# Layer 0's up-projection in seven products of halves instead of eight, and modulation units of 256 columns

## The chip, the cores and the metric

One core of one Trainium2 chip runs the kernel. Its engines are TensorE (PE in the rows; PEld is its weight load), VectorE (DVE), ScalarE (ACT), GpSimd (POOL) and SyncE (SP, which here issues DMAs). The metric is the device time of one execution in microseconds; the kernel before took 2715.18 us in the median of three runs (2710.06 to 2716.42).

## The reference

Two layers of a diffusion backbone in f32, on 512 latent and 256 context tokens with 1024 features. A layer modulates and norms the input, projects it, runs three mixers (mLSTM, attention, gated DeltaNet), merges them, and ends with a gated MLP. The change rewrites the first product of that MLP in layer 0:

```python
D_MODEL = 1024
D_FF = 2816
...
def conv_ffn(xn, w_up, conv_w, w_down):
    u = dwconv(xn @ w_up, conv_w)
    a, gt = jnp.split(u, 2, axis=-1)
    return (a * jax.nn.silu(gt)) @ w_down
...
        m_lat = jnp.split((silu_c @ ada_w[l] + ada_b[l])[:, None, :], 6, axis=-1)
```

`dwconv` is a convolution of width 3 along the tokens, on each sequence by itself. The last line is the modulation: a vector of 6 x 1024 values for a layer, for the latent tokens and for the context.

## The kernel before

Activations lie with features on the 128 partitions and tokens along the free axis, 768 of them in layer 0 (512 latent, 256 context) and 512 in layer 1's MLP. f32 products are made from pairs: each operand is split into a high part (`xh`, `wh`: ScalarE's cast to f32r) and a low one (`xl`, `wl`: what is left, VectorE's subtraction, L205), and TensorE adds three products, high by high, low by high and high by low (`mm3`, L248 to L250). `wsplit` makes the pair of a weight tile after `wraw` has loaded it through SP; raw tiles go round in a ring of three, pairs in a ring of two.

`ffn` (layer 0: names f0...) takes the 22 blocks of 128 hidden features in pairs. A unit f0g02 is the gate half of blocks 2 and 3 of group 0, f0a02 the other half of the same blocks; `gemm_fm` makes such a unit block by block: 8 row blocks of weights by 3 matmuls, each over 512 and over 256 tokens. The first unit, f0g00, goes its own way (`gemm_first`), f0a00 is the second and f0g02 the third. When a block is ready, `conv` takes it out of PSUM: ScalarE scales the middle tap (L1708), VectorE adds the two others (L1709, L1711, `scalar_tensor_tensor`). A gate block then gets silu (L1717); an a block is multiplied by its gate on GpSimd (L1723), cast to `gh` on ScalarE (L1724), and split to `gl` on VectorE (L1725). After four blocks the down-projection of the group (f0d0, f0d4, ...) follows one unit late: the order on TensorE is g00, a00, g02, a02, g40, d0, a40, g42, a42, g80, d4 and so on. It has eight output blocks, each of 4 row blocks by 3 matmuls by 512 and 256 tokens, and VectorE adds the result to the residual `hr` (L1743).

The modulation of layer 1 and of layer 0's MLP is made in units of 128 columns between other work (`ada_unit`): eight small matmuls of 32x128 into four row groups (`adp`, L467), a copy on ScalarE (`adr`, L470), and one unit later a transpose (`adc`, L489) and VectorE's sum (L491). 80 of the 96 units are made so. In layer 0's MLP sixteen of them follow the first blocks.

The order of the program is the scheduler's: it takes the instructions by priority and by an estimate of when they can start, each engine then runs its list in order, and semaphores make it wait. Weight loads and splits have a raised priority. GpSimd's and SP's lists are in order as well: what waits there holds back all behind it.

In the mLSTM a masked query `qz` is loaded for each tile of 128 tokens into one of two buffers, multiplied on GpSimd (L998) and read by the last matmuls of the tile (L1013).

```python
                        nc.vector.scalar_tensor_tensor(out=a[:, s + 1:e], in0=ps[:, 0:n - 1], scalar=w[0],
                                                       in1=a[:, s + 1:e], op0=ALU.mult, op1=ALU.add)
```

Here `ps` is a PSUM tile, so one of the two inputs lies in SBUF.

## Time and profile before

| | before |
|---|---|
| median of three runs | 2715.18 us |
| profiled execution, and its span | 2712.51 us, 2710.7 us |
| mean granted clock of TensorE | 0.994 |
| TensorE busy | 2640.8 us, 97% |
| VectorE, ScalarE, GpSimd busy | 1576.0, 1000.3, 267.0 us |
| chain that ended last | 84% TensorE, 7% DMA, 6% VectorE |
| layer 0's MLP | about 1012 to 1600 us of the span |

The busy share of TensorE says that its work makes the time; the table by stage says where it is full. A row of the timeline gives an instruction's start and duration in us; on TensorE durations overlap, since matmuls are pipelined, so the distance between two starts is what one costs. A duration on VectorE or GpSimd includes what the instruction waited after its semaphores had been met.

### The profile page before, as it was taken

Reading aid. Unit: us, or ns where it says so; the run is one execution under the profiler, and the core shown is the slowest. Engines: PE = TensorE matmul, PEld = TensorE weight load, DVE = VectorE, ACT = ScalarE, POOL = GpSimd, SP = SyncE. Lnnn points to the kernel's source line nnn. Section 1 sums busy time; section 2 is a strip of 40 time slices with the busy share of each in tenths; the row PEclk is TensorE's granted clock in tenths of the full one; section 3 lists DMA queues with packets and bytes.
Section 4 is the critical chain, followed back from the end, with each engine's and each line's share of the span. In section 5 each row is a group of like instructions: output and inputs, shape, how many; then the busy total and the mean of one; then the engine's idle time right before and its main releaser. Section 6 shows DMA issues by size and latency. Waiting matters only on the chain.

```text
span 2710.7 us, 46057 instructions
## 1 busy us (share of the span) xinstructions
PE 2640.8 (97%) x18041; PEld 2252.5 (83%) x18041; DVE 1576.0 (58%) x3517; ACT 1000.3 (37%) x2269; POOL 267.0 (10%) x262
## 2 busy tenths in 40 slices
...
DMA packets 526187, 344.29 MB, mean 127 GB/s; under 512 B 48167, under 2 KB 491281, under 8 KB 525201
## 3 DMA queue, kind: packets, MB, share of 16 engines
...
q8 instruction: 142, 2.33, 0.3%
...
q14 instruction: 76, 0.62, 0.1%
...
## 4 chain that ended last, share of the span: by engine, by line
PE 84%; DMA 7%; DVE 6%; ACT 1%; issue 1%; SPq 1%; POOL 0%; ACTq 0%; DVEq 0%; POOLq 0%
PE mg04p L248 2%; PE mg04p L250 2%; PE mg04p L249 2%; PE adp L467 2%; PE y0p L248 1%; PE y0p L249 1%; PE y0p L250 1%; PE mg14p L248 1%; PE mg14p L250 1%; PE mg14p L249 1%; PE y1p L248 1%; PE y0op L248 1%; PE y0op L250 1%; PE y0op L249 1%; PE y1p L249 1%
## 5 line engine op out<-in xcount | busy, mean ns | idle before, releaser
L1723 POOL TENSOR_TENSOR f0a<-f0a,f0g 128x768 f32<-128x768 f32 x22 | 40.6, 1848 | 486.4 <-DVE f0a L1711 486.4
L467 PE MATMUL adp<-ad,s 128*32 128x128 f32 x1280 | 66.8, 282 | 4.4 <-DVE cz0t L904 2.4
L1723 POOL TENSOR_TENSOR f1a<-f1a,f1g 128x512 f32<-128x512 f32 x22 | 28.5, 1294 | 313.3 <-DVE f1a L1711 303.5
L467 PEld LDWEIGHTS adp<-ad,s 128*32 128x32 f32 x1280 | 34.1, 109 | 28.1 <-issue 9.5
L1725 DVE TENSOR_TENSOR f0gl<-f0a,f0gh 128x768 fp32r<-128x768 f32 x22 | 21.1, 958 | 61.4 <-ACT f0gh L1724 61.3
L1724 ACT CAST f0gh<-f0a 128x768 fp32r<-128x768 f32 x22 | 18.4, 835 | 80.0 <-POOL f0a L1723 80.0
L1647 POOL TENSOR_TENSOR y0a<-y0a,y0g 128x768 f32<-128x768 f32 x16 | 33.0, 2063 | 128.0 <-DVE y0g L1644 125.7
L902 ACT ACTIVATE mg0t<-mg04p 128x512 f32<-128x512 f32 (+1 forms) x40 | 19.4, 486 | 40.6 <-PE mg04p L250 31.9
L470 ACT COPY adr<-adp 128x128 f32<-128x128 f32 x80 | 21.2, 265 | 33.4 <-PE adp L467 32.8
L1647 POOL TENSOR_TENSOR y1a<-y1a,y1g 128x512 f32<-128x512 f32 x16 | 23.9, 1494 | 75.6 <-DVE y1g L1644 75.3
L1717 ACT ACTIVATE f0g<-f0g 128x768 f32<-128x768 f32 x22 | 18.5, 846 | 32.9 <-DVE f0g L1711 32.9
L998 POOL TENSOR_TENSOR m0qz<-m0qz,m0e 64x512 f32<-64x512 f32 x12 | 15.4, 1282 | 151.9 <-DMA m0e<-g0rd 115.2
L1644 DVE SCALAR_TENSOR_TENSOR y0g<-y0g,y0p 128x512 f32<-128x512 f32 (+1 forms) x32 | 17.4, 550 | 15.4 <-PE y0p L250 14.6
L1717 ACT ACTIVATE f1g<-f1g 128x512 f32<-128x512 f32 x22 | 13.8, 632 | 32.9 <-DVE f1g L1711 32.9
L491 DVE TENSOR_REDUCE ada<-adc 128x2 f32<-128x8 f32 x80 | 12.9, 161 | 21.6 <-PE adc L489 21.3
L987 DVE SCALAR_TENSOR_TENSOR m0mb<-m0mb,g0a,cst 128x128 f32<-128x128 f32 x48 | 14.1, 346 | 18.7 <-DMA m0mb<-g0rd 18.6
L1668 DVE SCALAR_TENSOR_TENSOR hr<-y0op,y0gh,hr 128x512 f32<-128x512 f32 (+1 forms) x16 | 9.8, 615 | 21.1 <-PE y0op L250 21.1
L489 PE MATMUL adc<-cst,adr 128*128 128x128 f32 x80 | 21.9, 273 | 0.0
L1620 DVE TENSOR_TENSOR y0l<-y0ld,y0h 128x768 fp32r<-128x768 f32 x12 | 13.0, 1093 | 12.6 <-ACT y0h L1619 12.5
L1011 PE MATMUL m0n<-m0vb,m0mb 128*128 128x129 f32 x96 | 18.1, 279 | 1.2 <-issue 1.2
L1743 DVE SCALAR_TENSOR_TENSOR hr<-f0d4p,ada,hr 128x512 f32<-128x512 f32 (+1 forms) x16 | 9.9, 618 | 15.7 <-PE f0d4p L250 15.7
L1743 DVE SCALAR_TENSOR_TENSOR hr<-f0d8p,ada,hr 128x512 f32<-128x512 f32 (+1 forms) x16 | 9.9, 618 | 15.7 <-PE f0d8p L250 15.7
...
## 6 DMA issues: line engine op xcount, KB each, us to landing
...
```

The source lines that it names most:

```text
L248: nc.tensor.matmul(o, hv[:, k, :], xh[:, k, :], start=(k == 0), stop=False)
L249: nc.tensor.matmul(o, hv[:, k, :], xl[:, k, :], start=False, stop=False)
L250: nc.tensor.matmul(o, lv[:, k, :], xh[:, k, :], start=False, stop=(k == nk - 1))
L467: nc.tensor.matmul(ps[32 * j:32 * j + 32, 0:128], self.s32[:, 2 * k:2 * k + 32], raw[:, k, :], start=(k < 4), stop=(k >= 4), tile_position ...
L470: nc.scalar.copy(rw, ps[:, 0:128])
L489: nc.tensor.transpose(ps[:, 128:256], rw, self.ident)
L902: nc.scalar.activation(s, o, AF.Tanh, scale=0.5)
L1647: nc.gpsimd.tensor_tensor(out=a[:, :nt], in0=a[:, :nt], in1=gt[:, :nt], op=ALU.add)
L1717: nc.scalar.activation(a[:, :nt], a[:, :nt], AF.Silu)
L1723: nc.gpsimd.tensor_tensor(out=a[:, :nt], in0=a[:, :nt], in1=keep[b][:, :nt], op=ALU.mult)
L1725: nc.vector.tensor_tensor(out=gl[:, k, :nt], in0=a[:, :nt], in1=gh[:, k, :nt].bitcast(F32), op=ALU.subtract)
L1743: nc.vector.scalar_tensor_tensor(out=hv[:, a:b], in0=ps, scalar=self.ada[l][:, 40 + j, (a >= SEQ):(a >= SEQ) + 1], in1=hv[:, a:b], op0=ALU ...
```

## The change

`gemm7` makes a unit of two blocks from the third unit of layer 0 on (20 units). It cuts rows of the weights, the two blocks of columns and the tokens into halves and makes seven products of halves, each 4 row blocks by 3 matmuls by 384 tokens, in place of eight. The weights that go in are `w0` (the first block), `w1`, `w23` and `w4`: sums of halves that GpSimd makes from the two raw tiles r0 and r1 (`half`, L321 of the changed kernel: four of 128x512, two into s23, one over r1's first half, one into s4). ScalarE casts all four pairs, VectorE subtracts for w0, w23 and w1 (L225), GpSimd for w4. The inputs are quarters of `xh`, `xl` and four sums T1 to T4, which `norm_sums` makes once, after f0a00: GpSimd adds high and low again (four of 128x1536, L632), VectorE subtracts (four of 128x1536, L635), ScalarE casts and VectorE splits (L225); T2 is written over a quarter of `xh` and `xl`. The products go to PSUM tiles x1, x6, x7, x5, x1, x7, x5, the last three on top of what was there; ScalarE copies x1 (p1, and c0's first half), VectorE adds the rest (L355, L357, L359, L363, L365) into SBUF tiles c0 and c1, from which `conv` now reads. The order of the products in the program is x1, x6, x7, x5, x1, x7, x5.

Behind that: raw tiles go round in four buffers and pairs in three; the 128x3072 tiles of the merge and the MLP become 128x1536 tiles of one pool (`q6`); `xh` and `xl` are one tile over all tokens; the mLSTM's `qz` has one buffer; a modulation unit has 256 columns from two weight loads and follows every second block (`ada_next`). Layer 1's MLP keeps the plain units.

```diff
-        t = slot(nm) if slot else self.T([128, 1024], nm, tag="wraw", bufs=3)
+        t = slot(nm) if slot else self.T([128, 1024], nm, tag="wraw", bufs=4)
...
-            h = self.T([128, 1024], f"{nm}h", F32R, tag="wh", bufs=2)
-            l = self.T([128, 1024], f"{nm}l", F32R, tag="wl", bufs=2)
+            h = self.T([128, 1024], f"{nm}h", F32R, tag="wh", bufs=3)
+            l = self.T([128, 1024], f"{nm}l", F32R, tag="wl", bufs=3)
...
+    def gemm7(self, src, c0, x, nt, done, nm):
+
+
+        nc = self.nc
+        n = nt // 2
+        xh, xl, T = x
+        r0, r1 = [self.wraw(src[:, c0 + 128 * b:c0 + 128 * b + 128], KD, 128, f"{nm}r{b}") for b in range(2)]
+        s23 = self.pi.tile([128, KD, 128], F32, name=f"{nm}s23", tag="s23", bufs=2)
+        s4 = self.pi.tile([128, 4, 128], F32, name=f"{nm}s4", tag="s4", bufs=2)
+        lo, hi = slice(0, 4), slice(4, 8)
+
+        def half(out, a, b, op):
+            with self.high(self.prio):
+                nc.gpsimd.tensor_tensor(out=out, in0=a, in1=b, op=op)
+
+        half(s23[:, hi], r0[:, lo], r1[:, lo], ALU.subtract)
+        half(r1[:, lo], r1[:, lo], r1[:, hi], ALU.add)
+        half(s23[:, lo], r1[:, lo], r0[:, lo], ALU.subtract)
+        half(s4, r0[:, hi], s23[:, lo], ALU.subtract)
+        w0 = self.wsplit(r0, KD, 128, f"{nm}w0")
+        w23 = self.wsplit(s23, KD, 128, f"{nm}w23")
+        w1 = self.wsplit(r1, KD, 128, f"{nm}w1")
+        w4 = self.wsplit(s4, 4, 128, f"{nm}w4", nc.gpsimd)
+
+        def prod(ps, w, o, h, l, start, stop):
+
+            mm = lambda a, b, **kw: nc.tensor.matmul(ps, a, b, skip_group_check=True, **kw)
+            for k in range(4):
+                mm(w[0][:, o + k, :], h(k), start=(start and k == 0), stop=False)
+                mm(w[0][:, o + k, :], l(k), start=False, stop=False)
+                mm(w[1][:, o + k, :], h(k), start=False, stop=(stop and k == 3))
+
+        def of(k0, c):
+            return [lambda k, v=v: v[:, k0 + k, c] for v in (xh, xl)]
+
+        def oft(i):
+            return [lambda k, v=v: v[:, k, :] for v in T[i]]
+        t0, t1 = slice(0, n), slice(n, nt)
+        x1, x7 = self.pl(f"{nm}x1")[:, 0:n], self.pl(f"{nm}x7")[:, 0:n]
+        x6, x5 = self.pb(f"{nm}x6")[:, 0:n], self.pb(f"{nm}x5")[:, 0:n]
+        c = [self.st(f"{nm}c{b}") for b in range(2)]
+        u = self.st(f"{nm}u")
+        p1, u2, u3 = u[:, 0:n], u[:, n:2 * n], c[1][:, 0:n]
+        add = dict(op=ALU.add)
+        prod(x1, w0, 0, *of(0, t0), True, True)
+        nc.scalar.copy(p1, x1)
+        prod(x6, w23, 0, *oft(3), True, True)
+        nc.vector.tensor_tensor(out=u2, in0=x6, in1=p1, **add)
+        prod(x7, w23, 4, *oft(2), True, True)
+        nc.vector.tensor_tensor(out=u3, in0=x7, in1=u2, **add)
+        prod(x5, w1, 0, *oft(1), True, True)
+        nc.vector.tensor_tensor(out=c[1][:, t1], in0=x5, in1=u3, **add)
+        prod(x1, w0, 4, *of(4, t0), False, True)
+        nc.scalar.copy(c[0][:, t0], x1)
+        prod(x7, w1, 4, *oft(4), False, True)
+        nc.vector.tensor_tensor(out=c[1][:, t0], in0=x7, in1=u2, **add)
+        prod(x5, w4, 0, *of(4, t1), False, True)
+        nc.vector.tensor_tensor(out=c[0][:, t1], in0=x5, in1=u2, **add)
+        for b in range(2):
+            done(b, [(c[b][:, a:e], (a, e)) for a, e in ((0, SEQ), (SEQ, nt)) if e > a])
+            self.ada_next()
...
-        raw = self.wraw(self.I["ada_w"][l][:, 128 * g:128 * g + 128], KD, 128, f"ad{l}_{g}")
+        W = self.I["ada_w"][l]
+        raws = [self.wraw(W[512 * q:512 * q + 512, 256 * g:256 * g + 256], 4, 256, f"ad{l}_{g}_{q}") for q in range(2)]
         self.ada_fin()
         ps = self.adps[0](f"adp{l}_{g}")
-        for k in range(KD):
-            j = k % 4
-            nc.tensor.matmul(ps[32 * j:32 * j + 32, 0:128], self.s32[:, 2 * k:2 * k + 32], raw[:, k, :],
-                             start=(k < 4), stop=(k >= 4), tile_position=(0, 32 * j))
-        rw = self.T([128, 128], f"adr{l}_{g}", tag="adr")
-        nc.scalar.copy(rw, ps[:, 0:128])
+        for q, raw in enumerate(raws):
+            for j in range(4):
+                k = 4 * q + j
+                nc.tensor.matmul(ps[32 * j:32 * j + 32, 0:256], self.s32[:, 2 * k:2 * k + 32], raw[:, j, :],
+                                 start=(q == 0), stop=(q == 1), tile_position=(0, 32 * j))
+        rw = self.T([128, 256], f"adr{l}_{g}", tag="adr")
+        nc.scalar.copy(rw, ps[:, 0:256])
         self.adal = (l, g, rw)
...
+    def ada_next(self):
+
+        if self.nada:
+            self.nada -= 1
+            if self.nada % 2:
+                self.ada_unit()
+            if self.nada == 0:
+                self.ada_fin()
+
...
+        for b in range(2):
+            nc.tensor.transpose(ps[:, 256 + 128 * b:384 + 128 * b], rw[:, 128 * b:128 * b + 128], self.ident)
+        nc.vector.tensor_reduce(out=self.ada[l][:, 2 * g:2 * g + 2, :],
+                                in_=ps[:, 256:512].rearrange("p (o j r) -> p o r j", o=2, j=4)[:, :, 0:2, :],
                                 axis=AX.X, op=ALU.add)
...
+    def norm_sums(self):
+
+
+        nc, N = self.nc, self.N
+        nm, n = N["nm"], N["nt"] // 2
+        xh, xl = N["x"]
+        q = lambda v, k, t: v[:, 4 * k:4 * k + 4, n * t:n * t + n]
+        R = {}
+        for k, t in ((0, 0), (0, 1), (1, 1), (1, 0)):
+            R[k, t] = self.q6(f"{nm}R{k}{t}").rearrange("p (k t) -> p k t", k=4)
+            nc.gpsimd.tensor_tensor(out=R[k, t], in0=q(xh, k, t).bitcast(F32), in1=q(xl, k, t).bitcast(F32), op=ALU.add)
+
+        def sub(o, a, b):
+            nc.vector.tensor_tensor(out=R[o], in0=R[a], in1=R[b], op=ALU.subtract)
+        sub((0, 0), (0, 1), (0, 0))
+        sub((0, 1), (1, 1), (0, 1))
+        sub((1, 1), (1, 1), (0, 0))
+        sub((1, 0), (1, 0), (1, 1))
+        T = {}
+        for i, o in ((3, (1, 1)), (1, (0, 0)), (4, (1, 0)), (2, (0, 1))):
+            if i == 2:
+                T[i] = q(xh, 0, 1), q(xl, 0, 1)
+            else:
+                T[i] = [self.q6(f"{nm}T{v}{i}", F32R).rearrange("p (k t) -> p k t", k=4) for v in "hl"]
+            self.split(*T[i], R[o])
+        return xh, xl, T
...
-        qz = [self.P([128, 2, 4, 128], f"{nm}qz{i}", f"mqz{i}", 1) for i in range(2)]
-        for z in qz:
-            for d in range(2):
-                nc.gpsimd.memset(z[64 - 64 * d:128 - 64 * d, d], 0.0)
+        qd = self.P([128, 2, 4, 128], f"{nm}qz", "mqz", 1)
+        for d in range(2):
+            nc.gpsimd.memset(qd[64 - 64 * d:128 - 64 * d, d], 0.0)
         for tt in range(nt // 128):
             kT = self.b2([128, 4, 128], f"{nm}kTb{tt}")
-            qd = qz[tt % 2]
...
                 if f0 + p0 == 0:
                     self.gemm_first(KD, xs, done_g, f"{nm}g{f0}{p0}")
+                    x7 = None
+                elif x7:
+                    self.gemm7(U, D_FF + 128 * (f0 + p0), x7, nt, done_g, f"{nm}g{f0}{p0}")
                 else:
-                    self.gemm_fm(U, D_FF + 128 * (f0 + p0), 128 * n, KD, xs, done_g, f"{nm}g{f0}{p0}")
+                    self.gemm_fm(U, D_FF + 128 * (f0 + p0), 256, KD, xs, done_g, f"{nm}g{f0}{p0}")
                 if down and f0 + FG < NFF:
                     self.gemm_fm(*down)
                     down = None
-                self.gemm_fm(U, 128 * (f0 + p0), 128 * n, KD, xs, done_a,
-                             f"{nm}a{f0}{p0}")
-            segs = [((a, b), gh[:, :, a:b], gl[:, :, a:b]) for a, b in segb]
+                if x7:
+                    self.gemm7(U, 128 * (f0 + p0), x7, nt, done_a, f"{nm}a{f0}{p0}")
+                else:
+                    self.gemm_fm(U, 128 * (f0 + p0), 256, KD, xs, done_a, f"{nm}a{f0}{p0}")
+                    if f0 + p0 == 0 and nt == NT:
+                        x7 = self.norm_sums()
+            segs = [((a, b), Blocks(gh, a, b), Blocks(gl, a, b)) for a, b in segb]
```

**GpSimd where the first f0a blocks are multiplied.** Before, the products (f0a) follow the norm's sums (n01acc) and nothing lies between them:

```order
L546 TENSOR_TENSOR n01acc<-n01acc,n01sq_512_10916 128x256
L183 TENSOR_TENSOR n_512r<-n_512z,mhalf 128x2
L1723 TENSOR_TENSOR f0a_11324<-f0a_11324,f0g_11252 128x768
L1723 TENSOR_TENSOR f0a_11403<-f0a_11403,f0g_11260 128x768
L1723 TENSOR_TENSOR f0a_11645<-f0a_11645,f0g_11485 128x768
L1723 TENSOR_TENSOR f0a_11728<-f0a_11728,f0g_11565 128x768
```

After; r and s are raw tiles and sums of weights, n01R the rebuilt input:

```order
L321 TENSOR_TENSOR f0g02s_11222<-f0g02r_11220,f0g02r_11218 128x512
L1830 TENSOR_TENSOR f0a_11099<-f0a_11099,f0g_11027 128x768
L321 TENSOR_TENSOR f0g02s_11223<-f0g02r_11218,f0g02s_11222 128x512
L632 TENSOR_TENSOR n01R_11192<-n01xh,n01xl 128x1536
L632 TENSOR_TENSOR n01R_11194<-n01xh,n01xl 128x1536
L632 TENSOR_TENSOR n01R_11196<-n01xh,n01xl 128x1536
L632 TENSOR_TENSOR n01R_11198<-n01xh,n01xl 128x1536
L1830 TENSOR_TENSOR f0a_11182<-f0a_11182,f0g_11035 128x768
L321 TENSOR_TENSOR f0a02s_11381<-f0a02r_11377,f0a02r_11379 128x512
L225 TENSOR_TENSOR f0g02w4l<-f0g02s_11223,f0g02w4h 128x512
```

Between the first and the second product of f0a there are now a half for f0g02 and the four sums of 128x1536, and behind them the halves for f0a02 and the subtraction of w4.

**VectorE between f0a80 and the next units.** Before:

```order
L1709 SCALAR_TENSOR_TENSOR f0a_13170<-f0a80p_512_13145,vec,f0a_13170 128x255
L1711 SCALAR_TENSOR_TENSOR f0a_13170<-f0a80p_512_13145,vec,f0a_13170 128x255
L1725 TENSOR_TENSOR f0gl_12713<-f0a_13170,f0gh_12712 128x768
L1709 SCALAR_TENSOR_TENSOR f0a_13236<-f0a80p_0_13186,vec,f0a_13236 128x511
L1711 SCALAR_TENSOR_TENSOR f0a_13236<-f0a80p_0_13186,vec,f0a_13236 128x511
L205 TENSOR_TENSOR f0g82s1l<-f0g82r_13310,f0g82s1h 128x1024
L1709 SCALAR_TENSOR_TENSOR f0a_13236<-f0a80p_512_13211,vec,f0a_13236 128x255
L1711 SCALAR_TENSOR_TENSOR f0a_13236<-f0a80p_512_13211,vec,f0a_13236 128x255
L1725 TENSOR_TENSOR f0gl_12713<-f0a_13236,f0gh_12712 128x768
L1709 SCALAR_TENSOR_TENSOR f0g_13302<-f0g82p_0_13252,vec,f0g_13302 128x511
L1711 SCALAR_TENSOR_TENSOR f0g_13302<-f0g82p_0_13252,vec,f0g_13302 128x511
L205 TENSOR_TENSOR f0a82s0l<-f0a82r_13374,f0a82s0h 128x1024
```

After:

```order
L225 TENSOR_TENSOR f0g82w1l<-f0g82r_13047,f0g82w1h 128x1024
L1813 SCALAR_TENSOR_TENSOR f0a_13023<-f0a80c_12929,vec,f0a_13023 128x511
L1813 SCALAR_TENSOR_TENSOR f0a_13023<-f0a80c_12929,vec,f0a_13023 128x255
L1813 SCALAR_TENSOR_TENSOR f0a_13035<-f0a80c_12930,vec,f0a_13035 128x511
L1815 SCALAR_TENSOR_TENSOR f0a_13023<-f0a80c_12929,vec,f0a_13023 128x511
L1813 SCALAR_TENSOR_TENSOR f0a_13035<-f0a80c_12930,vec,f0a_13035 128x255
L1815 SCALAR_TENSOR_TENSOR f0a_13023<-f0a80c_12929,vec,f0a_13023 128x255
L1815 SCALAR_TENSOR_TENSOR f0a_13035<-f0a80c_12930,vec,f0a_13035 128x511
L355 TENSOR_TENSOR f0g82u<-f0g82x_13073,f0g82u 128x384
L1815 SCALAR_TENSOR_TENSOR f0a_13035<-f0a80c_12930,vec,f0a_13035 128x255
L357 TENSOR_TENSOR f0g82c_13076<-f0g82x_13072,f0g82u 128x384
L359 TENSOR_TENSOR f0g82c_13076<-f0g82x_13074,f0g82c_13076 128x384
```

The eight convolution steps of f0a80, which stood in pairs between the blocks, now stand in a row behind the last split of f0g82; in their midst is the sum L355 of f0g82, behind them L357 and L359.

## Rows read from the trace of the kernel before

**Rows 1.** The page's busy times (us, share of the span, instructions) and the chain by engine.

```profile
PE 2640.8 (97%) x18041; PEld 2252.5 (83%) x18041; DVE 1576.0 (58%) x3517; ACT 1000.3 (37%) x2269; POOL 267.0 (10%) x262
...
PE 84%; DMA 7%; DVE 6%; ACT 1%; issue 1%; SPq 1%; POOL 0%; ACTq 0%; DVEq 0%; POOLq 0%
```

**Rows 2.** By stage: stretch, length, busy PE PEld DVE ACT POOL, clock, DMA share, GB/s.

```profile
1160.00:1260.00 100.00, 100.00 (x572) 87.41 (x571) 46.80 (x68) 27.57 (x39) 7.38 (x4) 1.00 0.22 64
...
2060.00:2080.00 20.00, 17.78 (x374) 14.72 (x360) 16.17 (x47) 9.04 (x20) 1.42 (x2) 0.91 0.83 239
```

**Rows 3.** Timeline of TensorE in f0a02: start, duration, instruction.

```profile
1076.66 0.39 PE L249 MATMUL f0a02p<-n01xl,f0a02s0h 128*128 128x512 f32 x1
1076.89 0.39 PE L250 MATMUL f0a02p<-n01xh,f0a02s0l 128*128 128x512 f32 x1
1077.13 0.28 PE L248 MATMUL f0a02p<-n01xh,f0a02s0h 128*128 128x256 f32 x1
...
1077.37 0.28 PE L250 MATMUL f0a02p<-n01xh,f0a02s0l 128*128 128x256 f32 x1
```

**Rows 4.** Timeline of TensorE at a modulation unit, and at a run of 512 columns.

```profile
42.09 3.64 PE L438 MATMUL ad<-ad,s 128*32 128x512 f32 x32
...
1061.29 0.27 PE L489 MATMUL adc<-cst,adr 128*128 128x128 f32 x1
1061.49 0.64 PE L467 MATMUL adp<-ad,s 128*32 128x128 f32 x16
1062.06 0.50 PE L248 MATMUL f0g02p<-n01xh,f0g02s1h 128*128 128x512 f32 x1
```

**Rows 5.** VectorE's groups: names, shapes, count, busy us, mean ns, idle before.

```profile
L1725 DVE TENSOR_TENSOR f0gl<-f0a,f0gh 128x768 fp32r<-128x768 f32 x12 | 11.5, 958 | 35.0 <-ACT f0gh L1724 35.0
L1743 DVE SCALAR_TENSOR_TENSOR hr<-f0d4p,ada,hr 128x512 f32<-128x512 f32 x8 | 6.0, 751 | 10.4 <-PE f0d4p L250 10.4
L1743 DVE SCALAR_TENSOR_TENSOR hr<-f0d4p,ada,hr 128x256 f32<-128x256 f32 x8 | 3.9, 485 | 5.3 <-PE f0d4p L250 5.3
...
L205 DVE TENSOR_TENSOR f0g80s0l<-f0g80r,f0g80s0h 128x1024 fp32r<-128x1024 f32 x1 | 1.2, 1226 | 1.6 <-ACT f0g80s0h L204 1.6
```

**Rows 6.** GpSimd's groups, 900 to 1460 us, the same columns.

```profile
L1723 POOL TENSOR_TENSOR f0a<-f0a,f0g 128x768 f32<-128x768 f32 x16 | 29.6, 1847 | 363.3 <-DVE f0a L1711 363.3
...
L546 POOL TENSOR_TENSOR n01acc<-n01acc,n01sq 128x256 f32<-128x256 f32 x9 | 6.6, 736 | 15.2 <-ACT n01sq L545 9.5 <-DVE n01acc L546 4.5 <-DVE n_0t L619 1.2
L205 POOL TENSOR_TENSOR f0g00l<-f0g00r,f0g00h 128x1024 fp32r<-128x1024 f32 x2 | 4.8, 2400 | 37.0 <-ACT f0g00h L204 37.0
```

**Rows 7.** Timeline of VectorE and GpSimd in the merge, 900 to 920 us.

```profile
900.33 1.22 DVE L205 TENSOR_TENSOR y0s00l<-y0r,y0s00h 128x1024 fp32r<-128x1024 f32 x1
901.47 2.60 DVE L1620 TENSOR_TENSOR y0l<-y0ld,y0h 128x768 fp32r<-128x768 f32 x1
...
900.50 2.76 POOL L1647 TENSOR_TENSOR y0a<-y0a,y0g 128x768 f32<-128x768 f32 x1 [3.60 <-DVE y0g L1644]
...
916.38 2.77 DVE L205 TENSOR_TENSOR y0s20l<-y0r,y0s20h 128x1024 fp32r<-128x1024 f32 x1
...
916.15 1.91 POOL L1647 TENSOR_TENSOR y0a<-y0a,y0g 128x768 f32<-128x768 f32 x1 [1.84 <-DVE y0g L1644]
```

**Rows 8.** Timeline of both engines at the start of the span.

```profile
30.24 0.17 DVE L454 TENSOR_TENSOR ada<-ada,vec 128x8 f32<-128x8 f32 x1
30.33 2.33 DVE L503 SCALAR_TENSOR_TENSOR modA<-ada,vec 128x8 f32<-128x8 f32 x1
...
30.29 2.34 POOL L205 TENSOR_TENSOR c00ks0l<-c00kr,c00ks0h 128x1024 fp32r<-128x1024 f32 x1 [10.34 <-ACT c00ks0h L204]
```

**Rows 9.** Timeline at the third unit's start: GpSimd's first f0a product, TensorE's first matmul.

```profile
1047.65 1.85 POOL L1723 TENSOR_TENSOR f0a<-f0a,f0g 128x768 f32<-128x768 f32 x1 [32.38 <-DVE f0a L1711]
...
1052.70 0.50 PE L248 MATMUL f0g02p<-n01xh,f0g02s0h 128*128 128x512 f32 x1
```

**Rows 10.** GpSimd's mLSTM product: count, shortest, median, longest ns, first and last start.

```profile
L998 POOL TENSOR_TENSOR m0qz<-m0qz,m0e x12: 1263/1282/1326, 573.3 to 760.8; 64x512 f32<-64x512 f32 x12
```

134 lines of the change are left out of this document (65 added, 69 removed).

## The prediction

> **What bounds the kernel now.** I read the busy shares first, then the table by stage, then the single instructions. TensorE is busy 2640.8 of 2710.7 us and makes 84% of the chain that ended last [rows 1]. Layer 0's MLP, which the change rewrites, runs from about 1012 to 1600 us, and in 1160 to 1260 TensorE works 100.00 of 100 us at full clock, while VectorE has 46.80, ScalarE 27.57 and GpSimd 7.38 [rows 2]. So this stage is matmul time and nothing else: whatever takes matmuls away there is gained, as long as no other engine becomes late. That is what the rest of this text weighs, since the change buys fewer matmuls with more sums.
>
> **Products, the gain.** Two 128x512 matmuls start 0.2333 us apart, two 128x256 ones 0.12 (1076.66 to 1076.89, and 1077.13 to 1077.37 for two) [rows 3]. A plain call of 256 columns is 2 x 8 x 3 x (0.2333 + 0.12) = 16.96 us. A call by halves has seven products of 12 matmuls of 384 columns. No 384-column matmul is in the trace; between the two rows it is 0.1767 us (0.175 by the rate of 512, 0.18 by that of 256), so a call is 84 x 0.1767 = 14.84 us and a product 2.12. Ten pairs of g and a calls are changed, 20 calls: 20 x 2.12 = **-42.4 us** (-37 to -45).
>
> **Sums, the load on the other engines.** Per call VectorE makes three splits of 128x1024 at 1.23, five sums out of PSUM of 384 columns at about 0.62 (between 0.485 and 0.751), eight convolution steps at 0.75 or 0.48 (4.9) and on average one gl of 0.96 [rows 5]: 12.6 us of 14.84. GpSimd makes five sums of 128x512 (four halves and w4l) and on average one product of 128x768: between 0.736 for 256 columns, 1.848 for 768 and 2.400 for 1024 [rows 6], 512 columns are 1.29 and 1536 are 3.51, so 8.3 us of 14.84. Each engine alone fits. They don't fit beside each other as freely as that, though:
>
> **The two engines shut each other out.** At 900.50 GpSimd begins a 128x768 product that takes 2.76 us in place of 1.85; VectorE's split had started at 900.33. VectorE's next split, 0.96 alone, takes 2.60, and ends when GpSimd's product would be over plus its own 0.96. At 916.38 VectorE came second: 2.77 for a split of 1.23 while GpSimd lost nothing (1.91) [rows 7]. Whoever begins second waits for the whole instruction, and the one that waits comes next. A 128x8 scalar_tensor_tensor with both inputs in SBUF took 2.33 us inside GpSimd's split at 30.29, beside 0.17 for the instruction before it [rows 8], so the form of the convolution steps is stopped as well. In the plain units they read PSUM; in the new ones they read the sums c0 and c1 in SBUF. The Trainium skill (SBUF — State Buffer, section Who interferes with whom) states the same: a VectorE instruction with two SBUF inputs and a GpSimd instruction that reads SBUF share a read port under an exclusive lock, held for the whole instruction. Rows 7 and 8 agree; by that rule the sum below is -12 us, and without it (a plain walk of each engine) -39. Locked work per call is thus 3.7 + 4.9 + 0.96 of VectorE and 8.3 of GpSimd, 17.8 us, more than the call's 14.84 and than the plain 16.96. What saves it is that halves and splits of the next units are made behind the plain down-projections (33.9 us each, between groups of four calls).
>
> **The start of the products.** The third unit began at 1052.70 on TensorE, and GpSimd's first f0a product at 1047.65 [rows 9]. GpSimd's program there is: that product (to 1049.5), a half (1050.8), then four sums of 128x1536 that rebuild the normed input, 3.51 each; VectorE then subtracts and splits them (1.77 each by its rows, 0.96 for 768 and 1.23 for 1024). Walked with the lock, one instruction of each in turn: gl to 51.8, first sum to 55.3, w1l to 56.5, the next two sums to 63.5, a subtraction to 65.3, the last sum to 68.8, a subtraction, product f0a001, a subtraction, a half, the first split to 77.3, and so on alternately (w4l and halves) to the fourth T at 91.9. After its two products that need no T TensorE has nothing (from about 59) until 72, then pieces. The f0a02 product that stands before the last two needs f0a02w0l (94.4), and these end at 100.5. Without any wait: 1052.7 + 8 x 2.12 + 2.5 modulation units of 1.35 = 1073.1. Stall 27. If VectorE always went first the walk ends near 90 (17), without a lock at 82.7 (10). I take **+24**, near the alternation that rows 7 show, and with it the clock: after busy gaps the granted clock was 0.91 in 2060 to 2080 [rows 2], which costs 1 to 2 us there. Bounds +8 and +32.
>
> **The steady calls.** x7's second product waits for the VectorE sum of x7 and u2 (L357), due 10.6 us after a call's start, and in VectorE's order that sum stands behind eight convolution steps of the call before and its w1l split. From f0g82's start: GpSimd's half 0 to 1.3, w1l to 2.5, six steps to 6.5, GpSimd's product to 8.3, last step, L357 at 9.3: in time. Then w4l, f0a82's w0l (13.5), the second product (15.4), w23l (16.6), half, gl, half, w1l at 21.3, due 21.2; six steps with w4l between them, L357 of f0a82 at 28.2, due at 25.6: 2.6 us of TensorE lost. The first call after a down-projection has no convolution before it and loses nothing, nor does g120, behind which GpSimd has few halves. So about 2.8 for each of f0a42, f0a82, f0a122; f0a162, where the last group's four halves fall in the same stretch, about 6; a us each for f0a02 and f0a200: **+15** (0 if the gaps take GpSimd's work, +40 if every call loses 2).
>
> **Wide modulation units.** A unit of 128 columns costs 0.20 for the transpose (1061.29 to 1061.49) and 0.57 for its matmuls (to 1062.06), with the change back some 0.88 beside a plain unit. 32 records of 512 columns take 3.64 in one run, half of it for a group of 512 [rows 4], so 256 columns are about 0.98 in place of 2 x 0.57. With half as many changes of mode a pair saves 0.2 to 0.45, 40 pairs 8 to 18 us where TensorE is full. Most of them lie in the mixers, where they fill waits; some of those three that now stand in the start's stall cost nothing. **-11** (-4 to -20).
>
> **Small parts.** mLSTM's masked query has one buffer for two: its load for the next tile can only be issued by SP once the last matmul has read it, with what is queued on SP behind it held back, and then GpSimd's product of 1.28 [rows 10] lies between; 8 loads can lose a us, the mixers' fillers hide most: **+2** (-3 to +8). The deeper weight rings, the moved tails and the 128x1536 pool cost nothing that I can name: their waits in the order fall on instructions long done.
>
> **Sum.** 2712.5 (the profiled execution's own time) - 42.4 + 24 + 15 - 11 + 2 = 2700.1. The median of the runs shown is 2.7 above that execution, so 2703.
>
> **The rivals.**
> - *The lock costs little.* GpSimd's halves fall into VectorE's waits, VectorE is served first at the start: +14 and +3, modulation -13, rest +1: 2712.5 - 37.4 = 2675, with the 2.7 2678. For it: VectorE has 2.2 us free in a call and 3.1 us of PSUM sums, during which GpSimd may read. Against it: 8.3 us are to fit into 5.3.
> - *The lock takes the gain back (slower).* One mechanism: alternating with GpSimd stretches VectorE's row of eight steps before L357 in every call, so that x7's second product waits each time. With the start at 24 and the two small terms, the gain is gone at (42.4 + 11 - 24 - 2) / 20 = 1.4 us lost per call. Were VectorE stopped by all of GpSimd's time, a call would be 12.6 + 5.7 (GpSimd's share inside a group) = 18.3, 3.5 above 14.84. At 2.5 per call and a start of 30: -42.4 + 30 + 50 - 8 + 3 = +33, 2748; at 2.0 and 24, 2727. Against it: the first call of a group has no convolution beside it.
> - *The wide units bring nothing*, since they fill waits that stay: -12 becomes -1, 2714.
>
> **How the numbers follow.** Forecast as walked (2690 to 2716): 0.48. Lock cheap (2668 to 2690): 0.27. Gain taken back (2717 to 2750): 0.20. Wide units without effect (2708 to 2722): 0.05. A measurement of this kernel can tell about 0.3% from no change, 8.1 us: faster means below 2707, slower above 2723. The forecast case gives 0.29 faster and 0.19 same, the cheap one 0.27 faster, the third 0.01 same and 0.19 slower, the last 0.03 same and 0.02 slower: faster 0.56, same 0.23, slower 0.21. The range 2672 to 2736 leaves out a part of the two outer cases, about 0.15 in all; the likeliest one's own range is 2690 to 2716.
>
> **What would show it.** In the new trace: 384-column matmuls 0.177 us apart; a TensorE gap between about 1059 and 1072 and pieces until 1100 at f0g02; halves above 1.3 and f0a products above 1.85 us on GpSimd, splits above 1.23 on VectorE, side by side; waits of x7's second product for L357 in f0a42, f0a82, f0a122 and f0a162, not in the first call of a group; VectorE near 85% busy in the units. I am wrong if halves show 1.29 throughout (no lock in this form), if the four rebuilt sums end before 1066, or if the units run at 14.84 us without waits.

## The result

The changed kernel takes 2680.75 us in the median of its runs (2676.32 to 2683.99), the kernel before 2714.64 (2710.06 to 2716.42) beside it: a ratio of 0.9877, 95% interval 0.9857 to 0.9896, or 33.9 us less. The forecast of 2703 was 11.6 less than that median. Direction and range held; the size was a third of what came.

The profiled execution has a span of 2677.7 us. Busy times and chain of its page, which answer to [rows 1]:

```profile
PE 2584.4 (97%) x17161; PEld 2234.9 (83%) x17161; DVE 1699.3 (63%) x3605; ACT 1047.1 (39%) x2313; POOL 463.1 (17%) x362
...
PE 75%; DVE 10%; DMA 9%; issue 2%; ACT 1%; POOL 1%; SPq 1%; DVEq 0%; POOLq 0%; ACTq 0%
```

TensorE has 56 us less to do, but VectorE now makes 10% of the chain and DMA 9%. The stages that answer to [rows 2] (stretch, length, busy PE, PEld, DVE, ACT, POOL, clock, DMA share, GB/s):

```profile
1040.00:1045.00 5.00, 0.12 (x2) 0.00 (x0) 2.99 (x1) 0.43 (x1) 5.00 (x2) 0.85 0.90 272
1045.00:1065.00 20.00, 9.86 (x36) 6.43 (x37) 19.96 (x10) 6.90 (x6) 20.00 (x8) 0.50 0.22 63
...
1160.00:1260.00 100.00, 99.05 (x571) 94.43 (x570) 72.66 (x97) 40.99 (x60) 46.74 (x29) 1.00 0.23 65
```

In the steady stretch TensorE still works 99 of 100 us. At the start of the products it stands nearly still, and then runs at a granted clock of 0.50, its 1.2 GHz level: 20 us with 36 matmuls.

To find where time went I read, for every kernel, four marks on TensorE: the first matmul of f0g00 (the MLP's start), of f0g40 (the second group of units), of f0tp (the MLP's tail), and the span's end. One profile is uncertain by some 4 us in a stretch: e7_layout, whose ratio is 1, has 4.7 less than before ahead of f0g00; those of e11_qz1 and e17_narqz2 are of executions 6 and 7 us above the median of their runs.

| kernel | ratio to before (95%) | to f0g00 | f0g00 to f0g40 | f0g40 to f0tp | rest |
|---|---|---|---|---|---|
| before | 1 | 1012.2 | 77.9 | 481.2 | 1139.4 |
| changed | 0.9877 (0.9857 to 0.9896) | 993.3 | 101.6 | 444.0 | 1138.8 |
| e1_wide | 0.9948 (0.9931 to 0.9964) | 998.5 | 81.2 | 479.4 | 1139.7 |
| e2_narrow | 1.0004 (0.9991 to 1.0017) | 1017.3 | 101.4 | 445.5 | 1146.7 |
| e3_plain | 0.9913 (0.9894 to 0.9932) | 998.2 | 76.0 | 474.0 | 1144.3 |
| e12_plainnar | 1.0062 (1.0049 to 1.0074) | 1015.2 | 78.1 | 476.2 | 1155.2 |
| e11_qz1 | 1.0026 (1.0016 to 1.0036) | 1018.0 | 77.7 | 481.2 | 1146.2 |
| e17_narqz2 | 0.9998 (0.9986 to 1.0010) | 996.9 | 79.8 | 482.2 | 1157.2 |
| e18_widqz2 | 0.9976 (0.9963 to 0.9989) | 1008.4 | 76.7 | 476.1 | 1139.2 |
| e4_shallow | 0.9953 (0.9940 to 0.9966) | 995.7 | 78.1 | 474.2 | 1148.9 |
| e7_layout | 0.9996 (0.9984 to 1.0008) | 1007.5 | 78.0 | 481.1 | 1136.1 |
| e9_widelay | 0.9952 (0.9938 to 0.9967) | 997.1 | 79.0 | 479.4 | 1142.8 |
| e15_align | 0.9973 (0.9962 to 0.9984) | 1005.1 | 80.4 | 476.1 | 1142.7 |
| e5_early | 0.9831 (0.9812 to 0.9851) | 995.2 | 87.6 | 442.6 | 1140.4 |
| e6_vec | 0.9872 (0.9854 to 0.9890) | 992.9 | 97.2 | 443.8 | 1137.2 |
| e8_nohalves | 0.9775 (0.9755 to 0.9795) | 992.5 | 90.0 | 436.8 | 1129.5 |
| e13_halfvec | 0.9805 (0.9793 to 0.9818) | 996.4 | 89.0 | 444.1 | 1131.1 |
| e14_halfmix | 0.9836 (0.9823 to 0.9848) | 995.6 | 86.2 | 442.8 | 1138.5 |
| e16_best | 0.9938 (0.9924 to 0.9951) | 1004.9 | 94.3 | 459.5 | 1134.0 |
| e19_w4vec | 0.9794 (0.9776 to 0.9813) | 994.0 | 89.7 | 442.0 | 1131.4 |

Two things stand out at once in the second row. The start costs 23.7 us, close to the forecast's 24, though two of its calls are shorter now. And 18.9 us are gained before the first product, where the forecast had at most 9 (11 for the units, less 2), for the whole kernel.

**The start**, GpSimd's timeline and TensorE's waits in 1000 to 1110 us (us in all, times, longest), which answer to [rows 9]:

```profile
1031.14 2.27 POOL L321 TENSOR_TENSOR f0g02s<-f0g02r,f0g02s 128x512 f32<-128x512 f32 x1
1033.37 16.88 POOL L632 TENSOR_TENSOR n01R<-n01xh,n01xl 128x1536 f32<-128x1536 f32 x4
1050.21 3.41 POOL L1830 TENSOR_TENSOR f0a<-f0a,f0g 128x768 f32<-128x768 f32 x1
...
PE adp L541 <- DMA ad<-ada_w: 5.6, 2, 5.4
PE f0g02x L334 <- ACT n01xh L224: 4.4, 1, 4.4
PE f0g02x L334 <- ACT n01Th L224: 2.6, 1, 2.6
PE f0a02x L334 <- DVE f0a02w0l L225: 2.4, 1, 2.4
...
1053.51 0.69 PE L334 MATMUL f0g02x<-n01xh,f0g02w23h 128*128 128x384 f32 x1 [4.38 <-ACT n01xh L224]
...
1060.12 0.52 PE L334 MATMUL f0g02x<-n01xl,f0g02w23h 128*128 128x384 f32 x1
1060.44 0.52 PE L334 MATMUL f0g02x<-n01xh,f0g02w23l 128*128 128x384 f32 x1
```

The four rebuilt sums take 16.88 us; TensorE waits for the splits that stand behind them. The 5.4 us for a modulation unit's load had no place in the forecast, but they lie inside the gap that it drew: the product behind the units had to wait for `n01xh` until 1053.51 in any case. At the half clock, matmuls of 384 columns start 0.32 us apart.

**A steady call**: VectorE, GpSimd and TensorE's wait around f0a82, which starts at 1273.9.

```profile
1273.45 2.40 DVE L225 TENSOR_TENSOR f0a82w23l<-f0a82s,f0a82w23h 128x1024 fp32r<-128x1024 f32 x1
1275.77 2.04 DVE L1832 TENSOR_TENSOR f0gl<-f0a,f0gh 128x768 fp32r<-128x768 f32 x1
...
1278.21 1.84 DVE L225 TENSOR_TENSOR f0a82w1l<-f0a82r,f0a82w1h 128x1024 fp32r<-128x1024 f32 x1
1279.98 1.79 DVE L1813 SCALAR_TENSOR_TENSOR f0g<-f0g82c,vec,f0g 128x511 f32<-128x511 f32 x3
...
1284.67 0.54 DVE L357 TENSOR_TENSOR f0a82c<-f0a82x,f0a82u 128x384 f32<-128x384 f32 x1
...
1271.94 2.83 POOL L1830 TENSOR_TENSOR f0a<-f0a,f0g 128x768 f32<-128x768 f32 x1
1274.73 2.27 POOL L321 TENSOR_TENSOR f0g120s<-f0g120r,f0g120r 128x512 f32<-128x512 f32 x1
1277.08 1.90 POOL L321 TENSOR_TENSOR f0g120s<-f0g120r,f0g120s 128x512 f32<-128x512 f32 x1
1284.36 1.54 POOL L225 TENSOR_TENSOR f0a82w4l<-f0a82s,f0a82w4h 128x512 fp32r<-128x512 f32 x1 [5.38 <-ACT f0a82w4h L224]
...
1285.27 0.45 PE L334 MATMUL f0a82x<-n01Th,f0a82w1h 128*128 128x384 f32 x1 [0.74 <-DVE f0a82c L357]
```

This is the picture of [rows 7]: splits of 1.23 alone take 1.84 to 2.40 beside halves of 1.29 that take 1.90 to 2.27, and L357 comes late, as the walk said. But only 0.74 us late, not 2.6. Up to the end of w1l the walk was right: 21.3 us after f0g82's start, here 1280.2, and the row ends at 1280.05. Behind it two things differ. The eight steps and L355 take 4.7 us where the walk had 5.5, since in a row VectorE's instructions overlap (the row at 1279.98 is three steps, of 511, 255 and 511 columns: 1.79 in all, where [rows 5] give 0.75, 0.48 and 0.75). And w4l, which the walk put among the steps at 1.3 us, waits for ScalarE's cast and starts behind them.

### The profile page after: what moved, and what is told of

Read it like the earlier page. It is cut to its first block, busy times and chain, and to the rows that moved or that the text cites. A ratio compares the mean times of both kernels' runs of the same rounds, so it can differ in the third digit from the quotient of the medians.

```text
span 2677.7 us, 44644 instructions
## 1 busy us (share of the span) xinstructions
PE 2584.4 (97%) x17161; PEld 2234.9 (83%) x17161; DVE 1699.3 (63%) x3605; ACT 1047.1 (39%) x2313; POOL 463.1 (17%) x362
## 4 chain that ended last, share of the span: by engine, by line
PE 75%; DVE 10%; DMA 9%; issue 2%; ACT 1%; POOL 1%; SPq 1%; DVEq 0%; POOLq 0%; ACTq 0%
PE mg04p L265 1%; PE mg04p L266 1%; PE mg04p L264 1%; PE y0p L265 1%; PE y0p L264 1%; PE y0p L266 1%; PE adp L541 1%; PE mg14p L264 1%; PE mg14p L265 1%; PE mg14p L266 1%; PE y1p L264 1%; DMA m1mb<-g1rd 1%; PE y0op L264 1%; PE y0op L266 1%; PE y0op L265 1%
## 5 line engine op out<-in xcount | busy, mean ns | idle before, releaser
L541 PE MATMUL adp<-ad,s 128*32 128x256 f32 x640 | 55.7, 405 | 6.5 <-DMA ad<-ada_w 5.6
L1830 POOL TENSOR_TENSOR f0a<-f0a,f0g 128x768 f32<-128x768 f32 x22 | 51.9, 2360 | 57.8 <-DVE f0a L1815 53.4
L541 PEld LDWEIGHTS adp<-ad,s 128*32 128x32 f32 x640 | 18.5, 112 | 26.3 <-issue 14.2
L1832 DVE TENSOR_TENSOR f0gl<-f0a,f0gh 128x768 fp32r<-128x768 f32 x22 | 31.0, 1411 | 8.5 <-ACT f0gh L1831 8.5
L544 ACT COPY adr<-adp 128x256 f32<-128x256 f32 x40 | 14.8, 370 | 44.0 <-PE adp L541 42.8
L1107 POOL TENSOR_TENSOR m1qz<-m1qz,m1e 64x512 f32<-64x512 f32 x8 | 11.2, 1406 | 102.9 <-DMA m1mb<-g1rd 45.7
L1832 DVE TENSOR_TENSOR f1gl<-f1a,f1gh 128x512 fp32r<-128x512 f32 x22 | 15.1, 685 | 10.9 <-ACT f1gh L1831 10.7
L1831 ACT CAST f1gh<-f1a 128x512 fp32r<-128x512 f32 x22 | 13.5, 616 | 16.6 <-POOL f1a L1830 16.6
L1098 ACT ACTIVATE m0mb<-m0mb 128x512 f32<-128x512 f32 x12 | 7.6, 631 | 30.1 <-DVE m0mb L1096 25.4
```

The source lines that it names most:

```text
L541: nc.tensor.matmul(ps[32 * j:32 * j + 32, 0:256], self.s32[:, 2 * k:2 * k + 32], raw[:, j, :], start=(q == 0), stop=(q == 1), tile_positio ...
L1107: nc.gpsimd.tensor_tensor(out=qd[r, d], in0=qd[r, d], in1=e2[r], op=ALU.mult)
L1830: nc.gpsimd.tensor_tensor(out=a[:, :nt], in0=a[:, :nt], in1=keep[b][:, :nt], op=ALU.mult)
L1831: nc.scalar.copy(h, a[:, :nt])
L1832: nc.vector.tensor_tensor(out=gl[-1][:, b, :nt], in0=a[:, :nt], in1=h.bitcast(F32), op=ALU.subtract)
```

## Experiments

### The modulation units, and what they stand beside

e1_wide: the kernel before, with the new ada_unit and ada_fin alone.

```diff
-        raw = self.wraw(self.I["ada_w"][l][:, 128 * g:128 * g + 128], KD, 128, ...)
+        raws = [self.wraw(W[512 * q:512 * q + 512, 256 * g:256 * g + 256], 4, 256, ...) for q in range(2)]
```

> The kernel before with the wide modulation units alone (two loads of 128x4x256, eight 256-column matmuls, two transposes, the number of calls and groups halved); weight rings, products and everything else as before. Theory A: the 18.9 us that the changed kernel has gained before the MLP come from half as many changes between the matmuls of the projections and the small ones of the modulation: about 2697 (-15 to -20 against 2714.6), and f0g00 starts near 995. Rival B: they come from the deeper weight rings and the other order, and the units alone bring what the forecast gave them or less: 2706 to 2712 (-3 to -9).

0.9948, 14.1 us faster, 13.7 of them before f0g00: a little under theory A's range, well above rival B's. TensorE's groups in 180 to 850 us (count | busy us, mean ns | idle before), of before and of e1_wide:

```profile
L467 PE MATMUL adp<-ad,s 128*32 128x128 f32 x512 | 28.6, 280 | 3.6 <-DVE cz0t L904 2.4 <-ACT mg0t L902 1.2
L489 PE MATMUL adc<-cst,adr 128*128 128x128 f32 x32 | 8.7, 273 | 0.0
...
L470 PE MATMUL adp<-ad,s 128*32 128x256 f32 x256 | 21.6, 386 | 0.0
L493 PE MATMUL adc<-cst,adr 128*128 128x128 f32 x32 | 6.3, 272 | 0.0
```

256 matmuls take 21.6 us here where 512 took 28.6, and the transposes 2.4 less. That is 9.4 of the 13.7 us; that the changes between the two kinds of matmul are the cause was not tried apart.

e2_narrow: the changed kernel, with the old units.

> The changed kernel with the modulation units of 128 columns as before. Theory A (changeovers): 18 us slower than the changed kernel, about 2698, almost all of it before the MLP. Rival B (rings and order): 3 to 6 slower, 2684 to 2687. If the units inside the start of the products count too, a few us more lie between f0g02 and f0a02.

1.0004: both theories are far off. Without the wide units the whole gain is gone, 34.5 us (0.0127 of 2714.6), 24 of them before f0g00 and 8 in the last stretch. So the same edit is worth 14 alone and 34 here. Next come the rest of the edits without products.

e3_plain and e12_plainnar: the changed kernel without norm_sums, so that x7 stays None and every call is plain; e12_plainnar has the narrow units as well.

```diff
-                    if f0 + p0 == 0 and nt == NT:
-                        x7 = self.norm_sums()
```

> The changed kernel with plain products throughout (no rebuilt sums, no halves); wide units and rings stay. Theory A (from the milestones of the two traces: -13.5 us between the starts of f0g00 and the last tail, made of about -47 for 20 shorter calls, +27 at the start, +7 in the steady calls): 2681 + 14 = 2695, f0g00 to f0tp about 582 us in place of 568. Rival B: the calls lose more than the milestones say, since part of the MLP's gain comes from the rings (fewer weight waits): 2685 to 2690.

> The changed kernel with plain products and with modulation units of 128 columns: what is left are the rings, the tails, the smaller pools and the single query buffer. Theory A: the units are worth about 14 us wherever they stand, and the 33 that their undoing cost in the changed kernel come from the products' start (units waiting for their loads there): 2691 + 14 = 2705. Rival B: the units are worth more beside the deeper rings and the single query buffer (those cost the narrow units waits in the mixers): 2718 to 2725, f0g00 at 1015 or later.

e3_plain 0.9913 (2691.2 us, between theory A's 2695 and rival B's 2685 to 2690), e12_plainnar 1.0062: rival B, a little over its range. The units are worth 40 us beside the deeper weight rings and the single query buffer even where there is no product. From e3_plain to the changed kernel the products bring 9.8 us by the ratios (interval 2 to 17) and 4.4 by the marks inside the MLP (+25.6 at the start, -30.0 behind it); beside narrow units 15.7 and 7.4.

e11_qz1: the kernel before with one buffer for mLSTM's masked query.

```diff
-        qz = [self.P([128, 2, 4, 128], f"{nm}qz{i}", f"mqz{i}", 1) for i in range(2)]
+        qz = [self.P([128, 2, 4, 128], f"{nm}qz{i}", f"mqz{i}", 1) for i in range(1)]
```

> The kernel before with one buffer in place of two for mLSTM's masked query, nothing else. Forecast term: +2 (-3 to +8), from the load for the next tile behind the last matmul that reads the buffer and GpSimd's product of 1.28. Theory A: the waits of m0pt for m0hs (0 us before, 5.5 in the changed kernel) come from it: +3 to +6, 2715 to 2720. Rival B: those waits come from the order, the mixers' fillers hide the buffer: within 2 us of before.

+7.0 us: theory A by the time, a little over its range, and by the marks in both layers. By its wait it is not: m0pt's wait for m0hs stays near 0 here, and is 6.3 us in e12_plainnar but also 6.5 in e3_plain.

e17_narqz2 and e18_widqz2: e12_plainnar and e3_plain with two query buffers, for whose room the fourth raw weight buffer goes.

> The kernel with plain products and narrow units (e12_plainnar, +16.8 against before) with two buffers for mLSTM's masked query again; a raw weight buffer is given up for the room (three in place of four). Theory A: the single query buffer is what the rest of the edits cost (it alone is +7), and it is what makes the wide units worth 40 there in place of 14: 2714 to 2720. Rival B: the buffer is not it, the narrow units lose in the other order: 2726 to 2732.

> The kernel with plain products and wide units (e3_plain, ratio 0.9913) with two buffers for mLSTM's masked query and three raw weight buffers: the partner of e17_narqz2 (narrow, 0.9998), so that the difference is the worth of the wide units where the query buffer is double. Theory A: wide units are worth 40 us beside the single query buffer because they fill its waits with fewer pieces, and 14 beside the double one: ratio 0.994 to 0.996, 2694 to 2700. Rival B: they are worth as much with either buffer: 0.985 to 0.988, 2670 to 2680.

With narrow units the exchange wins 17 us back (1.0062 to 0.9998: theory A's way, and more than it said). With wide ones it loses 17 (0.9913 to 0.9976: neither theory). The units' worth falls to 6 us where the query buffer is double and the raw ring short. e4_shallow separates those two: e3_plain with rings of three raw and two split buffers, the query buffer single.

> The kernel with plain products and wide units of before (e3_plain, 2691), with the weight buffers back at three raw ones and two of each half; all else stays. The two runs with the normed input in one tile kept 0.120 us between 256-column matmuls, so the layout isn't what makes them 0.1135 in e3_plain. Theory A: the weights' buffers do (their number and so their addresses): 0.120 returns, MLP calls 16.85 in place of 16.5 (+7), time 2697 to 2701, as with units and layout alone. Rival B: the number of buffers does nothing, neither to the spacing nor to waits: 0.1135 and 2689 to 2693; what is left is the place of the other tiles.

0.9953: the time of theory A, but with rival B's spacing (below), so by another way. The rings are worth 10.9 us beside wide units (a wide unit takes two raw buffers at once). So with wide units the single query buffer costs nothing that shows (e4_shallow is no slower than e18_widqz2), with narrow ones 7 to 17. Why the mixers hide it in one case only I can't say: orders on all engines differ, and no single wait carries it.

### The 256-column matmuls

In e3_plain a plain call of the MLP takes 16.64 us from start to start in place of 16.96, with the same 96 matmuls: those of 256 columns, half of them, stand 0.1135 us apart in place of 0.120. Three kernels look for the cause. e7_layout and e9_widelay have one tile for the normed input, the second with wide units.

> The kernel before with one tile of 128x8x768 for the normed input (and for the merged one) in place of one of 512 and one of 256 columns, nothing else. In the kernel with wide units and plain products the 256-column matmuls stand 0.1135 us apart, in the kernel before and the one with wide units alone 0.120, those of 512 columns 0.2333 in all. Theory A: this comes from the layout of the normed input: 0.1135 here too, the plain calls of layer 0's MLP 16.5 in place of 16.85 (-7 over the MLP), with the projections of both layers 2702 to 2708. Rival B: it comes from the weights' buffers (three in place of two, at other addresses): 0.120 stays, and the time 2714.

> The kernel before with the wide modulation units and the one tile for the normed input; weight rings, mLSTM's two query buffers and all products as before. Theory A: units and layout make up all that the plain part of the changed kernel gained, and the deeper rings nothing: 2690 to 2693, as the kernel with plain products (2691.2). Rival B: the rings carry a part: 2695 to 2700. If the units are worth more beside the other edits (undone in the changed kernel they cost 35, alone they bring 14.5), this run shows whether the layout is the partner: then below 2688.

Rival B in both: 0.9996 and 0.9952, the calls stay at 16.96. e4_shallow above kept 16.64 with the old rings. What is left is the place of the tiles:

```diff
-        self.xss = self.T([128, 6], "xss")
+        self.xss = self.P([128, 6], "xss", "xss", 1)
-        self.xz, self.xr = self.T([128, 6], "xz"), self.T([128, 6], "xr")
+        self.xz, self.xr = self.P([128, 6], "xz", "xz", 1), self.P([128, 6], "xr", "xr", 1)
```

> The kernel before with three small tiles (128x6: xss, xz, xr) moved from the pool that lives through the whole kernel to the first stage's pool, as the changed kernel has them; everything else as before. It moves the address of every tile that is taken after them in the long-lived pool, the normed input and the split weights among them, by three times 24 bytes a row. Theory A: the 0.1135 us between 256-column matmuls in layer 0's MLP come from those addresses: 0.1135 here, plain calls of 16.5, the MLP 7 shorter, 2702 to 2707. Rival B: they come from another edit (pools inside the stage, buffers): 0.120 stays, and the time within 2 us of before.

0.9973, 7.4 us faster: theory A, though only 5.1 of it lie between f0g40 and f0tp. TensorE in f0a82 of e15_align (start, duration):

```profile
1292.45 0.28 PE L249 MATMUL f0a82p<-n01xl,f0a82s1h 128*128 128x256 f32 x1
1292.56 0.28 PE L250 MATMUL f0a82p<-n01xh,f0a82s1l 128*128 128x256 f32 x1
1292.67 0.28 PE L248 MATMUL f0a82p<-n01xh,f0a82s1h 128*128 128x256 f32 x1
```

Starts 0.11 apart, where [rows 3] have 0.12. But that holds from f0a80 on. In f0a40 to f0g80 of the same run the spacing is 0.118 (a call 16.84), as in e12_plainnar and e17_narqz2; with wide units it is 0.1135 there too. So the place of these tiles is a part of it and something that goes with the units another; which tile's address matters was not tried.

### The start of the products

e5_early issues the sums, subtractions and three splits ahead of f0a00's matmuls; e6_vec leaves them in place and puts the four sums on VectorE.

```diff
+                    rest = self.norm_sums() if nt == NT else None
...
-                        x7 = self.norm_sums()
+                        x7, rest = rest(), None
```

> The changed kernel with the rebuilt sums (four on GpSimd, the four subtractions and three of the four splits) issued before f0a00's matmuls; only the split that overwrites x follows behind them. Theory A: the 27 us stall at the start is GpSimd's chain of four sums of 4.25 us, begun at 1033, and GpSimd stands idle from 997 to 1025: the sums end near 1025, the stall falls to 5 to 10 us, and the time to about 2661 (2657 to 2666). Rival B: the stall is VectorE's row (subtractions, splits and weights alternating with GpSimd's halves at 2.8), which stays; the sums' earlier start brings 8 us at most: 2672 to 2676. Rival C: the sums and the normed input's own steps shut each other out, f0g00 becomes late and the gain is lost: 2681 or more.

> The changed kernel with the four rebuilt sums on VectorE in place of GpSimd, in the same place of the program (behind f0a00's matmuls). Theory A: the start's stall is the four sums of 4.25 us on GpSimd; on VectorE they take 1.74 each, and GpSimd's halves come earlier: stall 27 to about 17, time 2669 to 2673. Rival B: the stall is VectorE's row, to which this adds 7 us: 2681 to 2688.

e5_early 0.9831, 12.5 us under the changed kernel; the stretch to f0g40 falls from 101.6 to 87.6. Theory A in kind, at 2668.3 just over its range; 11.6 of the 25.6 us remain. GpSimd there, and the stretch 1040 to 1065:

```profile
1006.43 3.48 POOL L632 TENSOR_TENSOR n01R<-n01xh,n01xl 128x1536 f32<-128x1536 f32 x1 [7.13 <-DVE n01xl L735]
1015.79 3.47 POOL L632 TENSOR_TENSOR n01R<-n01xh,n01xl 128x1536 f32<-128x1536 f32 x1 [5.88 <-DVE n01xl L735]
1022.19 8.50 POOL L632 TENSOR_TENSOR n01R<-n01xh,n01xl 128x1536 f32<-128x1536 f32 x2 [2.94 <-DVE n01xl L735]
...
1040.00:1065.00 25.00, 20.22 (x116) 15.65 (x117) 20.88 (x21) 12.54 (x16) 20.26 (x10) 0.93 0.42 127
```

The sums end at 1030.7 in place of 1050.2, TensorE has 20.22 of 25 us, and the clock stays at 0.93. e6_vec, 0.9872, can't be told from the changed kernel and lies between its two theories: 4.4 us shorter at the start, where VectorE is busy without a gap from 1040 to 1065. As I read it, what GpSimd loses VectorE's row takes on. The place in the program decides, the engine hardly.

### The lock in the steady calls

e8_nohalves leaves out the four half sums of each call and uses raw weights of the same size, so that its products are not those of the reference.

```diff
-        half(s23[:, hi], r0[:, lo], r1[:, lo], ALU.subtract)
-        half(r1[:, lo], r1[:, lo], r1[:, hi], ALU.add)
-        half(s23[:, lo], r1[:, lo], r0[:, lo], ALU.subtract)
-        half(s4, r0[:, hi], s23[:, lo], ALU.subtract)
```

> The changed kernel without the four half sums of the weights per call on GpSimd: the weights that they should give are replaced by raw ones of the same size (the products are then not those of the reference), so splits, products and sums out of PSUM stay as many and as long. Theory A: what is left of stalls in the steady calls (7 us over 18 calls) and part of the start's comes from VectorE's splits and steps being shut out by the halves: steady calls at 14.5 without waits for L357 (there L353), the start 5 to 8 shorter: 2666 to 2670. Rival B: VectorE's own row is the bound in these calls, halves or not: the calls with 15.7 and 16.6 stay, 2676 to 2681.

Every steady call now takes 14.6 to 14.7 us from start to start; the changed kernel has 15.6 for f0a42, f0a82 and f0a122, 16.7 for f0a162, and 14.9 to 15.2 for the calls before these. From f0g40 to f0tp that is 444.0 to 436.8: **7.2 us are the halves' price there**, and at the start 11.6 more. Theory A in kind, and more than it said. (Of the whole 27.7 us another 9 lie in layer 1, where no instruction was taken out.) VectorE beside f0a82, which starts at 1259.1 here; L351 is the sum that L357 was:

```profile
1260.38 1.21 DVE L225 TENSOR_TENSOR f0a82w1l<-f0a82r,f0a82w1h 128x1024 fp32r<-128x1024 f32 x1
1261.51 1.80 DVE L1807 SCALAR_TENSOR_TENSOR f0g<-f0g82c,vec,f0g 128x511 f32<-128x511 f32 x3
...
1266.21 0.54 DVE L351 TENSOR_TENSOR f0a82c<-f0a82x,f0a82u 128x384 f32<-128x384 f32 x1
```

The split is back at 1.21 and the sum comes 7.1 us after the call's start, before 10.8.

e13_halfvec, e14_halfmix and e19_w4vec start from e5_early and put all halves, two of them, and all halves with w4l on VectorE.

```diff
-                nc.gpsimd.tensor_tensor(out=out, in0=a, in1=b, op=op)
+                nc.vector.tensor_tensor(out=out, in0=a, in1=b, op=op)
```

> The kernel with early rebuilt sums (e5_early, 2668) with the four half sums of each call on VectorE in place of GpSimd; w4l and the f0a products stay on GpSimd. Theory A: what remains of stalls (7 us in the steady calls, some 10 at the start) comes from VectorE being shut out by the halves (1.29 to 2.9 us on GpSimd): on VectorE they take about 0.62 each and shut nothing out, so steady calls near 14.6 and the time 2656 to 2662. Rival B: VectorE's row becomes the bound, 12.6 + 2.5 us for calls of 14.5: the second to fourth call of each group lose one to two us each, 2672 to 2685.

> The kernel with early sums (e5_early, ratio 0.9831) with two of the four half sums of a call on VectorE and two on GpSimd, in turn. Theory A (the lock: each half on GpSimd holds VectorE up to 1.3 us longer, each on VectorE costs it 0.62): between all on GpSimd and all on VectorE: 2662 to 2666. Rival B (each engine's load counts, not the lock): the even load is the best of the three: 2652 to 2657.

> The kernel with early sums and the halves on VectorE (e13_halfvec, ratio 0.9805) with the split w4l on VectorE too, so that GpSimd keeps only the f0a products beside the rebuilt sums. Theory A (the lock): 0.69 on VectorE in place of 1.3 to 2 during which VectorE is held: 2 to 6 us faster, ratio 0.978 to 0.980. Rival B (load: VectorE is at 82.6 of 100 us in 1160 to 1260 and stands in front of TensorE's sums): same or slower, 0.980 to 0.984.

e13_halfvec 0.9805, e19_w4vec 0.9794 (2658.85 us; not to be told from e13_halfvec, and both faster than both kernels: 0.0083, or 22.5 us, below the changed one by the ratios), e14_halfmix 0.9836, the same as e5_early and at theory A's upper edge. By time theory A holds for e13_halfvec and, within an interval that reaches into rival B's range, for e19_w4vec. The marks don't bear it out: the stretch f0g40 to f0tp is 442.6, 444.1, 442.8 and 442.0 in e5_early, e13, e14 and e19, and the gain lies in the last column, where TensorE waits 3.2 us for y1a in e5_early and hardly in the other two. VectorE of e13_halfvec, two halves and its load, and the load of e5_early:

```profile
1263.24 0.68 DVE L321 TENSOR_TENSOR f0g120s<-f0g120r,f0g120r 128x512 f32<-128x512 f32 x1
1264.03 0.69 DVE L321 TENSOR_TENSOR f0g120s<-f0g120r,f0g120s 128x512 f32<-128x512 f32 x1
...
1160.00:1260.00 100.00, 99.16 (x571) 94.30 (x569) 82.59 (x119) 39.44 (x59) 19.43 (x11) 1.00 0.24 69
...
1160.00:1260.00 100.00, 99.02 (x569) 94.09 (x568) 74.72 (x98) 40.82 (x60) 46.53 (x29) 1.00 0.22 64
```

A half costs 0.69 there, undisturbed; VectorE goes from 74.7 to 82.6 of 100 us. Within the products the halves cost 6 to 7 us against e8_nohalves on either engine: by the lock on one, by the load on the other, as I read it. What reorders layer 1 was not pursued.

e16_best is e13_halfvec with two query buffers and three raw ones.

> The kernel with early sums and the halves on VectorE (e13_halfvec, ratio 0.9805, 2659) with two buffers for mLSTM's masked query and three raw weight buffers in place of four. Theory A: the single buffer costs here what it costs alone, 7 us, most of it in the mixers of layer 1: 2651 to 2655. Rival B: with wide units its waits are filled, and the raw buffer is missed in layer 1 (rings of three, two and two cost the plain kernel 11): 2660 to 2668.

0.9938, 36 us slower: far beyond rival B. 15.4 of them lie between f0g40 and f0tp, where the second calls of the groups take 18.7 us in place of 15.2. TensorE's matmul in f0g42 with its wait, and VectorE just before:

```profile
1186.42 0.44 PE L334 MATMUL f0g42x<-n01Th,f0g42w1h 128*128 128x384 f32 x1 [2.25 <-DVE f0g42c L357]
...
1175.42 0.69 DVE L321 TENSOR_TENSOR f0a42s<-f0a42r,f0a42r 128x512 f32<-128x512 f32 x1 [1.10 <-DMA f0a42r<-w_up]
...
1185.22 0.68 DVE L321 TENSOR_TENSOR f0a42s<-f0a42r,f0a42s 128x512 f32<-128x512 f32 x1
1185.82 0.55 DVE L357 TENSOR_TENSOR f0g42c<-f0g42x,f0g42u 128x384 f32<-128x384 f32 x1
```

A call holds two raw buffers until w0, w1 and s4 are made. With three the next call's second load can't be issued early, its halves are made inside the call before, and L357 stands behind them. So the fourth raw buffer, bought with the query's second one, is worth more than it cost. Where the other 21 us come from was not pursued.

## Why the prediction was wrong in size

Along one path from before to changed, by the ratios:

| step | run | measured | forecast |
|---|---|---|---|
| wide units | e1_wide | -14.1 | -11 |
| tile addresses | e15_align | -7.4 | none |
| other plain edits | e3_plain less the two above | -2.1 | +2 |
| products with all their waits | changed less e3_plain | -9.8 | -42.4 + 24 + 15 = -3.4 |
| sum | | -33.4 | -12.4 |

The second and third line assume that e1_wide and e15_align add up, which no run of both alone shows.

Of the 21 us that the forecast missed, 14.6 lie in the first three lines, which hold no product: 9 forecast, 23.6 measured. The other 6.4 are within the interval of two ratios, and the marks don't put them into the MLP: there the products bring 4.4 us where 3.4 were forecast. That this came out is luck in part, since two of its terms were wrong and cancel.

- **Wide units, -11, and small parts, +2: the step that failed.** They measured -14.1 and, with the moved tiles, -9.5. The units lie inside their bounds when alone. They were priced apart from the single query buffer and the rings, though: beside those they carry 34 to 40 us. The single query buffer costs 7 in the kernel before, near the top of its bounds, and nothing that shows beside wide units. That the deeper rings "cost nothing that I can name" left out that they give 10.9 beside wide units. And moving three tiles of 24 bytes a row was in the change and had no term: it gives 7.4. Why the units and the query buffer bear on each other stays open.
- **Products, -42.4.** Matmuls of 384 columns start 0.17 us apart (TensorE in f0g80):

```profile
1200.08 0.33 PE L334 MATMUL f0g80x<-n01Th,f0g80w23l 128*128 128x384 f32 x1
1200.25 0.33 PE L334 MATMUL f0g80x<-n01Th,f0g80w23h 128*128 128x384 f32 x1
1200.42 0.34 PE L334 MATMUL f0g80x<-n01Tl,f0g80w23h 128*128 128x384 f32 x1
```

  f0g80 to f0d4 is 14.63 us for 84 of them, 0.174 each: just below the lower bound of 0.175. With 256 columns at 0.1135 the mean of the two rows would have been 0.173. Against e3_plain's plain calls (16.64 from start to start) a call saves 2.01, forecast 2.12.
- **The start, +24.** The reason was right, GpSimd's sums and the alternation, and the walk was close. f0g02 began at 1034.15, 18.55 before the walk's 1052.70. In the walk's time the last rebuilt sum ended at 68.8, as it said, the product behind the gap began at 72.1 (72), the last T was split at 89.5 (91.9), and f0g02 ended at 99.4 (100.5). The size was a little low. The stretch grew by 23.7 against before and 25.6 against e3_plain although its two changed calls are 2.0 to 2.3 shorter each, so the waits and the slow clock cost 28 to 30 there. The clock was priced at 1 to 2 us. Some 36 matmuls stand 0.32 apart in place of 0.174, which is up to 5 us, an estimate and an upper bound, since part of them had time before the next operand came.
- **The steady calls, +15.** Places and wait were right (L357 in f0a42, f0a82, f0a122, f0a162), the size was double: 7.2 by e8_nohalves, for the two reasons given at f0a82 above. The rule cited from the Trainium skill (SBUF — State Buffer, section Who interferes with whom) held: in the changed kernel's MLP halves and splits shut each other out wherever they meet (splits of 1.22 alone take up to 3.1 us, halves of 1.29 up to 2.8). But most don't meet: the median half takes 1.30 there, the median split 1.23.
- **Rivals.** "The lock costs little" gave 2678, nearest to the time, but not its way: the start was not cheap. "The lock takes the gain back" fell, with 0.4 us lost per call (7.2 over 18) where it needed 1.4. "The wide units bring nothing" is refuted by e1_wide and e2_narrow.
- **Signs of being wrong.** None of the three came: halves took up to 2.8 us, the sums ended behind 1066 in the walk's time, and the units had waits. VectorE was 76 to 79% busy in the units of a group (f0a80 to f0d8: 79), not near 85.
